# Gate and up of two feed-forward networks as a 2x2 block product by seven products

## The chip, the core and the metric

The kernel runs on one NeuronCore of a Trainium2 chip. Its engines are TensorE (PE in the profile; its weight loads are PEld), VectorE (DVE), ScalarE (ACT), GpSimd (POOL) and SyncE (SP, which here issues DMAs). Each has its own queue and works it in order. The metric is the time on the device in microseconds.

## The reference

One layer of a decoder for 512 tokens of 1024 features, in float32:

```python
x = x + 0.5 * RMSNorm(SwiGLU_1(RMSNorm(x)))
x = x + RMSNorm(mixer(RMSNorm(x)))        # attention and mLSTM, merged by gates
x = x + 0.5 * RMSNorm(SwiGLU_2(RMSNorm(x)))

def swiglu(x, w_gate, w_up, w_down):
    return (jax.nn.silu(x @ w_gate) * (x @ w_up)) @ w_down
```

w_gate and w_up are 1024 x 2816, w_down is 2816 x 1024. The change is in the two SwiGLUs.

## The kernel before

All runs on one core in program order: the first feed-forward network (a in the names), the mixer, the second one (b). Tokens lie along the free axis: hT holds the normed input, 1024 features as 8 chunks of 128 partitions by 512 tokens. Float32 accuracy is made from three products of rounded parts: each operand is split into a high part (h) and the rest (l), and xh·wh, xl·wh and xh·wl are added in PSUM.

`load_w` (L70 to L78) brings one weight tile of 128 x 1024 in: a DMA on SP's queue into wf (3 buffers), the high part wh by a cast on ScalarE (L75), the low part wl by a subtraction on VectorE (L77); wh and wl have 5 buffers each. `ws` (L165) makes one 128 x 512 output with 24 matmuls of 512 columns (8 chunks, three terms).

`ffn` runs over 22 blocks of 128 columns of gate and up. The first two (EARLY) go through `by_halves` (L175), in halves of 256 tokens, because the later tokens' norm is still under way. Each other block loads gate and up, runs `ws` for each, and `close` takes silu of gate on ScalarE (L228) and multiplies with up on VectorE (L229) into aT. Then `down` multiplies aT (split by `get_x` into ah, L250, and al, L251) with w_down, 22 steps of `step` (L215 to L217), and the post norm follows. GpSimd makes the power -1/2 of the norms (L89), a few masks at the start, and some DMAs.

The order of the work is that of the program as its scheduler places it by each tile's dependences; a tile with a number of buffers is free again when its last reader is done.

Of the kernel before, what the change touches and what calls it, by code (L numbers as in the profile page):

```python
# [39 lines left out]
def tile_hybrid_block(ctx: ExitStack, tc: tile.TileContext, a: dict):  # L40
# [180 lines left out]

    def ffn(pool, low, todo, first_w, hT, wgu, wd, post, finish, name, later=None, pins=()):
        hTh, hTl = hT
        aT = pool.tile([P, NF, T], F32, name=f"aT_{name}")

        def close(f, pg):
            s = pool.tile([P, T], F32, tag="s", bufs=2, name=f"s_{name}{f}")
            nc.scalar.activation(s, pg[0], AF.Silu)  # L228
            nc.vector.tensor_tensor(aT[:, f, :], pg[1], s, op=ALU.mult)  # L229
        early = []  # L230
        for f in range(EARLY):
            wg, wu = first_w if first_w and f == 0 else [load_w(wgu[f, b], f"{name}gu{f}{b}", after=pins if f + b else ()) for b in range(2)]
            early.append((wg, wu, pair(f"pg_{name}{f}")))
        by_halves([(pg, (wg, wu)) for wg, wu, pg in early], hTh, hTl, todo)
        for f in range(EARLY):
            close(f, early[f][2])
        if later:
            later()
# [15 lines left out]
        return down(pool, NF, lambda kk: wd[kk], get_x, post, finish, todo, name)  # L254


    with tc.tile_pool(name="low_a", bufs=1) as la, tc.tile_pool(name="ffn_a", bufs=1) as fa:
        hbuf = [(act, "h"), (fa, "h2")]
        tbuf = [(act, "tmp"), (fa, "tmp2")]
# [620 lines left out]
```

## Time and profile before

| | |
|---|---|
| median of 3 runs | 1408.47 us (1407.61 to 1408.63) |
| the profiled execution | 1408.52 us, its span 1406.7 us |
| busy TensorE, its weight loads | 99%, 84% |
| busy VectorE, ScalarE, GpSimd | 44%, 35%, 2% |
| mean granted clock of TensorE | 0.998 of full |

The busy shares are means over the whole span. A stretch is read by its own rows: how often a step comes back, and what ended each engine's idle time before it.

### The profile page before, as it was taken

What the parts mean: (1) busy time and instruction counts of PE and PEld (TensorE: products, weight loads), DVE (VectorE), ACT (ScalarE), POOL (GpSimd) and SP (SyncE); (2) the same over time, 40 slices, a digit from 0 to 9 for tenths busy, and PEclk for the clock granted to TensorE, in tenths of its full rate; (3) what the DMA queues carried; (4) which work ended last, traced back from release to release, by engine and by line L of the source; (5) the groups of instructions that cost most, each with busy time, mean ns of one, the idle gap of its engine ahead of it and who ended that gap; (6) DMA issues with size and microseconds to landing.
All of it is one profiled execution on the core that took longest, in us unless ns stands there. A gap on an engine that the chain in (4) does not pass through costs nothing.

```text
span 1406.7 us, 16599 instructions
## 1 busy us (share of the span) xinstructions
PE 1392.6 (99%) x6752; PEld 1185.3 (84%) x6752; DVE 625.0 (44%) x986; ACT 486.7 (35%) x761; POOL 29.1 (2%) x52
## 2 busy tenths in 40 slices
PE   8999999999999999999999999999999999999998
PEld 8888888888899889988888888888888888888886
DVE  5332222333773675565756753333374323222333
ACT  5322222222533533344445443222254222222322
POOL 1000000000100000000000000000010000000000
PEclk9999999999999999999999999999999999999999
DMA  6433333333143222222222232333323333323321
GB/s 234 126 90 100 96 102 92 93 103 91 46 121 115 90 76 75 75 75 75 75 87 78 75 118 78 90 101 95 105 76 120 91 104 90 103 92 97 99 75 60
DMA packets 37357, 133.12 MB, mean 95 GB/s; under 512 B 4268, under 2 KB 4268, under 8 KB 37280
## 3 DMA queue, kind: packets, MB, share of 16 engines
q1 hardware_dynamic: 36144, 128.50, 29.9%
q0 software_dynamic: 1136, 3.56, 0.8%
q8 instruction: 53, 0.87, 0.2%
q14 instruction: 24, 0.20, 0.0%
HBM read 129.95 MB, written 2.10 MB: 94 GB/s over the span
## 4 chain that ended last, share of the span: by engine, by line
PE 96%; DVE 1%; issue 1%; ACT 1%; DMA 0%; POOL 0%; SPq 0%; POOLq 0%; DVEq 0%; ACTq 0%
PE pg_b L165 15%; PE pg_a L165 15%; PE p L165 11%; PE pq L165 7%; PE pm L165 6%; PE acc_b L216 3%; PE acc_b L215 3%; PE acc_b L217 3%; PE acc_a L216 2%; PE acc_a L215 2%; PE acc_a L217 2%; PE pvo L602 2%; PE pvo L604 2%; PE pvo L603 2%; PE pg_a L175 2%; PE pq L175 2%
## 5 line engine op out<-in xcount | busy, mean ns | idle before, releaser
L215 PE MATMUL acc_a<-wh_ad,ah_a 128*128 128x512 f32 x176 | 68.6, 390 | 0.0
L217 PE MATMUL acc_a<-wl_ad,ah_a 128*128 128x512 f32 x176 | 68.5, 389 | 0.0
L216 PE MATMUL acc_a<-wh_ad,al_a 128*128 128x512 f32 x176 | 68.5, 389 | 0.0
L215 PE MATMUL acc_b<-wh_bd,ah_b 128*128 128x512 f32 x176 | 68.5, 389 | 0.0
L216 PE MATMUL acc_b<-wh_bd,al_b 128*128 128x512 f32 x176 | 68.5, 389 | 0.0
L217 PE MATMUL acc_b<-wl_bd,ah_b 128*128 128x512 f32 x176 | 68.5, 389 | 0.0
L165 PE MATMUL pq<-hTh_mx,wh_qk 128*128 128x512 f32 x160 | 63.5, 397 | 0.0
L165 PE MATMUL pq<-hTl_mx,wh_qk 128*128 128x512 f32 x160 | 62.4, 390 | 0.0
L165 PE MATMUL pg_a<-hTl_f,wh_ag 128*128 128x512 f32 x160 | 62.3, 389 | 0.0
L165 PE MATMUL pg_b<-hTl_f,wh_bg 128*128 128x512 f32 x160 | 62.3, 389 | 0.0
L165 PE MATMUL pg_a<-hTh_f,wh_ag 128*128 128x512 f32 x160 | 62.3, 389 | 0.0
L165 PE MATMUL pg_b<-hTh_f,wh_bg 128*128 128x512 f32 x160 | 62.3, 389 | 0.0
L165 PE MATMUL pg_a<-hTh_f,wh_au 128*128 128x512 f32 x160 | 62.2, 389 | 0.0
L165 PE MATMUL pg_a<-hTl_f,wh_au 128*128 128x512 f32 x160 | 62.2, 389 | 0.0
L165 PE MATMUL pg_b<-hTh_f,wh_bu 128*128 128x512 f32 x160 | 62.2, 389 | 0.0
L165 PE MATMUL pg_b<-hTl_f,wh_bu 128*128 128x512 f32 x160 | 62.2, 389 | 0.0
L77 DVE TENSOR_TENSOR wl_ad<-wf_ad,wh_ad 128x1024 fp32r<-128x1024 f32 x22 | 26.9, 1225 | 69.4 <-ACT wh_ad L75 69.4
L77 DVE TENSOR_TENSOR wl_bd<-wf_bd,wh_bd 128x1024 fp32r<-128x1024 f32 x22 | 26.9, 1225 | 69.4 <-ACT wh_bd L75 69.4
L77 DVE TENSOR_TENSOR wl_au<-wf_au,wh_au 128x1024 fp32r<-128x1024 f32 x20 | 24.5, 1226 | 69.7 <-ACT wh_au L75 63.6
L77 DVE TENSOR_TENSOR wl_bu<-wf_bu,wh_bu 128x1024 fp32r<-128x1024 f32 x20 | 24.5, 1226 | 69.7 <-ACT wh_bu L75 62.3
L229 DVE TENSOR_TENSOR aT_a<-pg_a,s_a 128x512 f32<-128x512 f32 x22 | 15.2, 691 | 85.3 <-PE pg_a L165 84.6
L229 DVE TENSOR_TENSOR aT_b<-pg_b,s_b 128x512 f32<-128x512 f32 x22 | 15.2, 691 | 84.6 <-PE pg_b L165 84.6
(339 smaller groups left out, 3432.9 us busy)
## 6 DMA issues: line engine op xcount, KB each, us to landing
wf_qk<-in_wqk SPq DMA_DIRECT2D x24, 512.0 KB, 3.6
wf_ad<-in_wd SPq DMA_DIRECT2D x22, 512.0 KB, 3.6
wf_bd<-in_wd SPq DMA_DIRECT2D x22, 512.0 KB, 3.6
wf_ag<-in_wgu SPq DMA_DIRECT2D x20, 512.0 KB, 3.6
wf_au<-in_wgu SPq DMA_DIRECT2D x20, 512.0 KB, 3.6
wf_bg<-in_wgu SPq DMA_DIRECT2D x20, 512.0 KB, 3.7
wf_bu<-in_wgu SPq DMA_DIRECT2D x20, 512.0 KB, 3.6
wf_mqk<-in_wmqk SPq DMA_DIRECT2D x16, 512.0 KB, 3.6
```

The source lines that it names most:

```text
L77: nc.vector.tensor_tensor(wl, wf, wh.bitcast(F32), op=ALU.subtract)
L165: nc.tensor.matmul(out, lhsT=wt[:, k * P:(k + 1) * P], rhs=x[:, k, tok], start=n == 0, stop=n == len(terms) - 1)
L175: nc.tensor.matmul(outs[b][:, tok], lhsT=ws_[b][w][:, k * P:(k + 1) * P], rhs=x[:, k, tok], start=i + k + hf == 0, stop=hf == 1 and i == 2 ...
L215: nc.tensor.matmul(out, lhsT=xh[:, tk], rhs=wh[:, cs], start=first, stop=False)
L216: nc.tensor.matmul(out, lhsT=xl[:, tk], rhs=wh[:, cs], start=False, stop=False)
L217: nc.tensor.matmul(out, lhsT=xh[:, tk], rhs=wl[:, cs], start=False, stop=last)
L229: nc.vector.tensor_tensor(aT[:, f, :], pg[1], s, op=ALU.mult)
L602: nc.tensor.matmul(out, lhsT=hTh[:, k, tk], rhs=wh[:, cs], start=k == 0, stop=False)
L603: nc.tensor.matmul(out, lhsT=hTl[:, k, tk], rhs=wh[:, cs], start=False, stop=False)
L604: nc.tensor.matmul(out, lhsT=hTh[:, k, tk], rhs=wl[:, cs], start=False, stop=k == KD - 1)
```

## The change

In blocks 4 to 21 of both networks (36 blocks) gate and up together become one 2x2 block product. One block's gate and up are the rows, two halves of the 1024 features are the inner blocks, and two halves of the 512 tokens the columns. Instead of 8 block products, 7 are made of sums of the weight blocks and sums of the token blocks. A product is 12 matmuls of 256 columns (4 chunks, three terms; `product`). I call them P1 to P7 by the number k in `product`; `g` and `u` are the weight tiles of a block, `a` to `d` their sums.

`token_parts` makes the sums of token blocks once per network, during block 2, in the part of aT that is written later. Per block, `front` has GpSimd make two sums (`ab`), `sums` has VectorE make two more (`cd`), and `take` splits each into h and l as `load_w` does: w1 and w2 from g, w4 from half of u, w6 and w3 from cd, w7 and w5 from ab. In the texts, wl12, wl4, wl63 and wl75 are the subtractions on VectorE for them. After the products VectorE joins them: `uv` (two sums in one), three `z`, and the product into aT; ScalarE copies `q1` and takes silu in two halves of 256 columns (silu0, silu1). Buffers: ab, cd, uv and s 1, z, q1 and w4 2, the other weights 5 as before. `Order` fixes the order on VectorE, ScalarE and GpSimd to the order of the calls. P4 of a block runs one turn late, between P5 and P2 of the next block. The gains' loads come after the blocks, and silu's s has 1 buffer.

```diff
@@ -219,44 +230,224 @@
+    Q = KD // 2 * P
+    H = T // 2
+    ADD, SUB, MUL = ALU.add, ALU.subtract, ALU.mult
...
+    class Order:
+        def __init__(self):
+            self.last = {}
+
+        def __call__(self, eng, fn, *args, **kw):
+            with tc.issue_after(self.last[eng]) if eng in self.last else nullcontext():
+                self.last[eng] = getattr(getattr(nc, eng), fn)(*args, **kw).ins
+
+    def token_parts(low, tmp, hTh, hTl, name):
+        def quad(t, i, j):
+            return t[:, 4 * i:4 * i + 4, j * H:(j + 1) * H]
+
+        hf, xs_ = tmp[:, 0:8, :], tmp[:, 8:16, :]
+        for j in (1, 0):
+            for i in (1, 0):
+                nc.vector.tensor_tensor(quad(hf, i, j), quad(hTh, i, j).bitcast(F32), quad(hTl, i, j).bitcast(F32),
+                                        op=ADD)
+        b11, b12, b21, b22 = (quad(hf, i, j) for i in range(2) for j in range(2))
+        f = {k: xs_[:, 2 * i:2 * i + 2, :].rearrange("p a (b c) -> p (a b) c", c=H) for i, k in enumerate((5, 6, 7, 4))}
+        parts = {1: (quad(hTh, 0, 0), quad(hTl, 0, 0)), 2: (quad(hTh, 1, 0), quad(hTl, 1, 0)),
+                 3: (quad(hTh, 1, 1), quad(hTl, 1, 1))}
+
+        def part(k):
+            xh, xl = (low.tile([P, 4, H], F32R, name=f"x{k}{x}_{name}") for x in "hl")
+            split(f[k], xh, xl)
+            parts[k] = (xh, xl)
+
+        nc.vector.tensor_tensor(f[5], b11, b12, op=SUB)
+        nc.vector.scalar_tensor_tensor(f[6], f[5], -1.0, b22, op0=MUL, op1=SUB)
+        part(6)
+        part(5)
+        nc.vector.tensor_tensor(f[7], b22, b12, op=SUB)
+        part(7)
+        nc.vector.scalar_tensor_tensor(f[4], f[6], -1.0, b21, op0=MUL, op1=SUB)
+        part(4)
+        return parts
+
+    def seven(fs, wgu, x, low, scr, aT, name):
+        do = Order()
+        tt = lambda out, p, q, op: do("vector", "tensor_tensor", out, p, q, op=op)
+        cast = lambda out, p: do("scalar", "copy", out, p)
+
+        class Unit:
+            def __init__(self, f):
+                self.f, self.n, self.w = f, f"{name}{f}", {}
+
+            def load(self):
+                self.gu = []
+                for b in range(2):
+                    t = act.tile([P, 2, Q], F32, tag="wf", bufs=3, name=f"{'gu'[b]}_{self.n}")
+                    nc.sync.dma_start(t, wgu[self.f, :, b * 1024:(b + 1) * 1024].rearrange("p (q c) -> p q c", c=Q))
+                    self.gu.append(t)
+
+            def take(self, keys, src, n=2):
+                pool, tag, bufs = (wpool, "", 5) if n == 2 else (low, "4", 2)
+                wh, wl = (pool.tile([P, n, Q], F32R, tag=f"w{y}{tag}", bufs=bufs, name=f"w{y}{keys[0]}_{self.n}")
+                          for y in "hl")
+                for i, k in enumerate(keys):
+                    self.w[k] = (wh[:, i, :], wl[:, i, :])
+                cast(wh, src)
+                return lambda: tt(wl, src, wh.bitcast(F32), SUB)
+
+            def front(self):
+                g, u = self.gu
+                self.ab = scr.tile([P, 2, Q], F32, tag="ab", bufs=1, name=f"ab_{self.n}")
+                do("gpsimd", "tensor_tensor", self.ab[:, 0, :], g[:, 0, :], u[:, 0, :], op=ADD)
+                do("gpsimd", "tensor_tensor", self.ab[:, 1, :], u[:, 0, :], u[:, 1, :], op=ADD)
+                self.low12 = self.take((1, 2), g)
+
+            def sums(self):
+                g, u = self.gu
+                cd = scr.tile([P, 2, Q], F32, tag="cd", bufs=1, name=f"cd_{self.n}")
+                low4 = self.take((4,), u[:, 1:2, :], 1)
+                tt(cd[:, 0, :], self.ab[:, 0, :], u[:, 1, :], ADD)
+                tt(cd[:, 1, :], cd[:, 0, :], g[:, 1, :], ADD)
+                self.lowcd = self.take((6, 3), cd)
+                low4()
+
+            def product(self, out, k, first, last):
+                (wh, wl), (xh, xl) = self.w[k], x[k]
+                terms = [(wh, y, i) for i in range(4) for y in (xh, xl)] + [(wl, xh, i) for i in range(4)]
+                for n, (wt, y, i) in enumerate(terms):
+                    nc.tensor.matmul(out, lhsT=wt[:, i * P:(i + 1) * P], rhs=y[:, i, :], start=first and n == 0,
+                                     stop=last and n == len(terms) - 1, skip_group_check=True)
+
+            def open(self):
+                n = self.n
+                self.pa, self.pb = bank(f"qa_{n}"), bank(f"qb_{n}")
+                self.q1 = scr.tile([P, H], F32, tag="q1", bufs=2, name=f"q1_{n}")
+                self.uv = scr.tile([P, 2, H], F32, tag="uv", bufs=1, name=f"uv_{n}")
+                self.z = scr.tile([P, 3, H], F32, tag="z", bufs=2, name=f"z_{n}")
+                self.s = scr.tile([P, 2, H], F32, tag="s", bufs=1, name=f"s_{n}")
+                self.a, self.b, self.c = self.pa[:, 0:H], self.pb[:, 0:H], self.pb[:, H:T]
+
+            def inner(self):
+                tt(self.z[:, 1, :], self.b, self.uv[:, 1, :], ADD)
+                tt(self.z[:, 2, :], self.c, self.uv[:, 0, :], ADD)
+
+            def silu(self, i):
+                do("scalar", "activation", self.s[:, i, :], self.z[:, 2, :] if i else self.a, AF.Silu)
+
+            def finish(self):
+                self.product(self.b, 4, False, False)
+                tt(self.z[:, 0, :], self.b, self.q1, ADD)
+                do("vector", "scalar_tensor_tensor", aT[:, self.f, :].rearrange("p (a b) -> p a b", b=H),
+                   self.z[:, 0:2, :], -1.0, self.s, op0=MUL, op1=MUL)
+
+        us = [Unit(f) for f in fs] + [None, None]
+        us[0].load()
+        us[0].front()
+        us[1].load()
+        us[0].low12()
+        us[0].sums()
+        us[0].lowcd()
+        us[0].take((7, 5), us[0].ab)()
+        us[1].front()
+        prev = None
+        for i in range(len(fs)):
+            u, v, w = us[i:i + 3]
+            u.open()
+            if prev:
+                prev.inner()
+                prev.silu(1)
+            u.product(u.a, 1, True, False)
+            cast(u.q1, u.a)
+            if v:
+                v.low12()
+            u.product(u.b, 6, True, False)
+            if w:
+                w.load()
+            if v:
+                v.sums()
+            u.product(u.c, 5, False, False)
+            tt(u.uv, u.pb.rearrange("p (a b) -> p a b", b=H), u.q1[:, None, :].broadcast_to([P, 2, H]), ADD)
+            if v:
+                v.lowcd()
+            if prev:
+                prev.finish()
+            u.product(u.a, 2, False, True)
+            u.silu(0)
+            if v:
+                v.take((7, 5), v.ab)()
+            u.product(u.b, 7, False, False)
+            u.product(u.c, 3, False, True)
+            if w:
+                w.front()
+            prev = u
+        prev.inner()
+        prev.silu(1)
+        prev.finish()
+
+    PLAIN = 4
...
-            s = pool.tile([P, T], F32, tag="s", bufs=2, name=f"s_{name}{f}")
...
-        for f in range(EARLY, NF):
-            wg = load_w(wgu[f, 0], f"{name}g{f}")
-            wu = load_w(wgu[f, 1], f"{name}u{f}")
-            pg = pair(f"pg_{name}{f}")
-            ws(pg[0], wg, KD, hTh, hTl)
-            ws(pg[1], wu, KD, hTh, hTl)
-            close(f, pg)
...
+            x = None
+            for f in range(EARLY, PLAIN):
+                w = load_plain(f)
+                if f == EARLY:
+                    x = token_parts(low, aT[:, NF - 16:, :], hTh, hTl, name)
+                pg = pair(f"pg_{name}{f}")
+                for b in range(2):
+                    ws(pg[b], w[b], KD, hTh, hTl)
+                close(f, pg)
+            seven(range(PLAIN, NF), wgu, x, low, scr, aT, name)
+
+        dn = ExitStack()
+        dlow = dn.enter_context(new_pool(f"low_{name}", "left"))
+        work.pool = dn.enter_context(new_pool(f"dn_{name}"))
+        if begin:
+            begin()
...
-        r[f"wgu{i}"] = np.stack([cols(f(f"{n}_w_gate")), cols(f(f"{n}_w_up"))], 1)
+        r[f"wgu{i}"] = np.concatenate([cols(f(f"{n}_w_gate")), cols(f(f"{n}_w_up"))], 2)
```

Three places of the new order. First VectorE in the middle of the first network, before: two weight subtractions and a product per block (ag9 is gate of block 9).

```order
L229 TENSOR_TENSOR aT_a_204<-pg_a6_1_724,s_a6_773 128x512
L77 TENSOR_TENSOR wl_ag9_910<-wf_ag9_906,wh_ag9_908 128x1024
L77 TENSOR_TENSOR wl_au9_916<-wf_au9_912,wh_au9_914 128x1024
L229 TENSOR_TENSOR aT_a_204<-pg_a7_1_789,s_a7_838 128x512
L77 TENSOR_TENSOR wl_ag10_975<-wf_ag10_971,wh_ag10_973 128x1024
```

The same engine and place now, one turn (wl1 is wl12, wl6 is wl63, wl7 is wl75; a7 to a9 are blocks):

```order
L247 TENSOR_TENSOR wl7_a8_1090<-ab_a8_993,wh7_a8_1089 128x1024
L247 TENSOR_TENSOR z_a7_1003<-qb_a7_1000,uv_a7_1002 128x256 x2
L247 TENSOR_TENSOR wl1_a9_1121<-g_a9_1034,wh1_a9_1120 128x1024
L247 TENSOR_TENSOR cd_a9_1162<-ab_a9_1117,u_a9_1036 128x512
L247 TENSOR_TENSOR cd_a9_1162<-cd_a9_1162,g_a9_1034 128x512
L247 TENSOR_TENSOR wl4_a9_1164<-u_a9_1036,wh4_a9_1163 128x512
L247 TENSOR_TENSOR uv_a8_1126<-qb_a8_1124,q1_a8_1125 128x512
L247 TENSOR_TENSOR wl6_a9_1169<-cd_a9_1162,wh6_a9_1168 128x1024
L247 TENSOR_TENSOR z_a7_1003<-qb_a7_1000,q1_a7_1001 128x256
L247 SCALAR_TENSOR_TENSOR aT_a_205<-z_a7_1003,s_a7_1004 128x512
L247 TENSOR_TENSOR wl7_a9_1214<-ab_a9_1117,wh7_a9_1213 128x1024
```

Each turn had three operations, and now has eleven: weight work of block 9 and the joining of blocks 7 and 8 alternate. Next ScalarE over the same turn, with what each row waits for (the s read from qa is silu0, that from z silu1):

```order
L247 ACTIVATE s_a7_1004<-qa_a7_999 128x256 [waits DVE_49,PE_49,Activation_49]
L247 CAST wh7_a8_1089<-ab_a8_993 128x1024 [waits Pool_49]
L247 CAST wh1_a9_1120<-g_a9_1034 128x1024 [waits DMAHW7_49,PE_49]
L247 ACTIVATE s_a7_1004<-z_a7_1003 128x256 [waits DVE_49]
L247 COPY q1_a8_1125<-qa_a8_1123 128x256 [waits PE_49]
L247 CAST wh4_a9_1163<-u_a9_1036 128x512 [waits DMAHW0_49,PE_49]
L247 CAST wh6_a9_1168<-cd_a9_1162 128x1024 [waits DVE_49]
```

Before, a turn was two casts and one silu. silu0 waits for VectorE, since s has one buffer and aT of the block before reads it; the cast of w4 waits for TensorE, since w4 has two. GpSimd, which had nothing to do in this stretch:

```order
L247 TENSOR_TENSOR ab_a8_993<-u_a8_912 128x512
L247 TENSOR_TENSOR ab_a9_1117<-g_a9_1034,u_a9_1036 128x512 [waits DMAHW7_49,DMAHW0_49,DVE_49]
L247 TENSOR_TENSOR ab_a9_1117<-u_a9_1036 128x512
```

The first add of a block waits for VectorE, the last reader of ab, which is wl75 of the block before. Last, VectorE at the end of the first network's blocks (d2 to d4 are weights of `down`, a21 is the last block):

```order
L88 TENSOR_TENSOR wl_ad2_2936<-wf_ad2_2932,wh_ad2_2934 128x1024
L88 TENSOR_TENSOR wl_ad3_2970<-wf_ad3_2966,wh_ad3_2968 128x1024
L247 TENSOR_TENSOR z_a21_2729<-qb_a21_2726,uv_a21_2728 128x256 x2
L88 TENSOR_TENSOR wl_ad4_3004<-wf_ad4_3000,wh_ad4_3002 128x1024
L247 TENSOR_TENSOR z_a21_2729<-qb_a21_2726,q1_a21_2727 128x256
L247 SCALAR_TENSOR_TENSOR aT_a_205<-z_a21_2729,s_a21_2730 128x512
L438 TENSOR_TENSOR al_a0_2853<-aT_a_205,ah_a0_2852 128x512
```

Weights of down stand between the last block's steps, and al of step 0 stands behind them all; before, al of the first steps was made early, among the blocks.

## Rows read from the trace of the kernel before

**Rows 1.** The page's head, busy time of each engine, and its chain by engine.

```profile
span 1406.7 us, 16599 instructions
PE 1392.6 (99%) x6752; PEld 1185.3 (84%) x6752; DVE 625.0 (44%) x986; ACT 486.7 (35%) x761; POOL 29.1 (2%) x52
...
PE 96%; DVE 1%; issue 1%; ACT 1%; DMA 0%; POOL 0%; SPq 0%; POOLq 0%; DVEq 0%; ACTq 0%
```

**Rows 2.** Timeline, VectorE: start, length (us), engine, line, operation, tiles, count.

```profile
49.29 0.69 DVE L229 TENSOR_TENSOR aT_a<-pg_a,s_a 128x512 f32<-128x512 f32 x1 [4.23 <-PE pg_a L165]
49.90 1.22 DVE L77 TENSOR_TENSOR wl_ag<-wf_ag,wh_ag 128x1024 fp32r<-128x1024 f32 x1
51.03 0.69 DVE L251 TENSOR_TENSOR al_a<-aT_a,ah_a 128x512 fp32r<-128x512 f32 x1
...
60.17 0.69 DVE L229 TENSOR_TENSOR aT_a<-pg_a,s_a 128x512 f32<-128x512 f32 x1 [4.23 <-PE pg_a L165]
...
71.05 0.69 DVE L229 TENSOR_TENSOR aT_a<-pg_a,s_a 128x512 f32<-128x512 f32 x1 [4.22 <-PE pg_a L165]
```

**Rows 3.** Windows: busy us (count) of PE, PEld, DVE, ACT, POOL; clock, DMA.

```profile
20.00:40.00 20.00, 20.00 (x163) 19.66 (x162) 11.59 (x14) 10.51 (x14) 0.34 (x1) 1.00 0.52 162
50.00:70.00 20.00, 20.00 (x90) 16.57 (x89) 6.59 (x7) 6.42 (x8) 0.00 (x0) 1.00 0.34 106
```

**Rows 4.** Timeline, TensorE, the halves of the first two blocks.

```profile
30.43 2.08 PE L175 MATMUL pg_a<-hTh_f,wl_agu 128*128 128x256 f32 x16
32.35 2.08 PE L175 MATMUL pg_a<-hTh_f,wh_agu 128*128 128x256 f32 x16
```

**Rows 5.** Groups by form, VectorE: busy us, mean ns, then idle before.

```profile
L755 DVE SCALAR_TENSOR_TENSOR t<-t,p 128x512 f32<-128x512 f32 x16 | 11.0, 688 | 42.7 <-PE p L165 42.7
L612 DVE TENSOR_TENSOR vml<-pvo,vmh 128x256 fp32r<-128x256 f32 x16 | 6.7, 420 | 0.0
```

**Rows 6.** Groups by form, ScalarE.

```profile
L75 ACT CAST wh_au<-wf_au 128x1024 fp32r<-128x1024 f32 x18 | 18.9, 1047 | 70.3 <-PE pg_a L165 70.3
L250 ACT CAST ah_a<-aT_a 128x512 fp32r<-128x512 f32 x20 | 12.3, 615 | 4.7 <-DVE aT_a L229 4.7
...
L676 ACT ACTIVATE jm<-po,dn 128x256 f32<-128x256 f32 x16 | 7.5, 472 | 4.3 <-DVE dn L673 4.1
L611 ACT CAST vmh<-pvo 128x256 fp32r<-128x256 f32 x16 | 6.0, 373 | 2.3 <-PE pvo L604 2.2
```

**Rows 7.** Timeline, TensorE, the end of block 2.

```profile
47.66 1.52 PE L165 MATMUL pg_a<-hTh_f,wl_au 128*128 128x512 f32 x6
```

**Rows 8.** Timeline, VectorE and TensorE, the first transposes.

```profile
6.58 0.75 DVE L129 SCALAR_TENSOR_TENSOR h_f<-x,r_f,g_f1pre 128x512 f32<-128x512 f32 x1 [0.93 <-DMA g_f1pre<-in_ffn_pre_g]
...
7.47 0.63 PE L137 MATMUL pt_f<-ident,h_f 128*128 128x128 f32 x4 [1.57 <-DVE h_f L129]
```

**Rows 9.** Timeline, GpSimd, the start.

```profile
0.24 0.10 POOL L869 MEMSET const-float32-0.0<- 128x1 f32 x1 [0.24 <-issue]
...
0.74 0.20 POOL masks.py:197 MEMSET ident<- 128x128 f32 x1 [0.29 <-POOLq L869]
1.02 0.29 POOL masks.py:199 TENSOR_SCALAR_AFFINE_SELECT ident<-ident 128x128 f32<-128x128 f32 x1
```

**Rows 10.** Timeline, VectorE and GpSimd, the post norm of the first network.

```profile
360.08 0.16 DVE L100 SCALAR_TENSOR_TENSOR v_pf<-sp_f 128x1 f32<-128x1 f32 x1 [2.09 <-ACT jk_pf L96]
360.15 0.69 DVE L154 TENSOR_TENSOR fg_f<-acc_a,g_f1post 128x512 f32<-128x512 f32 x1
...
360.40 0.56 POOL L89 TENSOR_TENSOR r_pf<-v_pf,nhalf 128x1 f32<-128x1 f32 x1 [340.06 <-DVE v_pf L100]
```

**Rows 11.** Timeline, VectorE, the last pre norm before the mixer.

```profile
383.45 0.15 DVE L100 SCALAR_TENSOR_TENSOR v_mx<-ss_mx 128x1 f32<-128x1 f32 x1
383.52 1.21 DVE L77 TENSOR_TENSOR wl_qk<-wf_qk,wh_qk 128x1024 fp32r<-128x1024 f32 x1
385.18 0.49 DVE L117 TENSOR_SCALAR h_mx<-h_mx,r_mx 128x512 f32<-128x512 f32 x1 [0.44 <-POOL r_mx L89]
```

**Rows 12.** Timeline, GpSimd, the same place.

```profile
383.68 1.46 POOL L89 TENSOR_TENSOR r_mx<-v_mx,nhalf 128x1 f32<-128x1 f32 x1 [4.91 <-DVE v_mx L100]
```

**Rows 13.** Timeline, TensorE, from the last block to down.

```profile
254.83 1.07 PE L165 MATMUL pg_a<-hTh_f,wl_au 128*128 128x512 f32 x4
255.74 0.39 PE L215 MATMUL acc_a<-wh_ad,ah_a 128*128 128x512 f32 x1
```

**Rows 14.** DMA issues: count, KB each, median us to landing.

```profile
wf_ag<-in_wgu SPq DMA_DIRECT2D x20, 512.0 KB, 3.6
```

More of the change, by code (lines that the diff above doesn't have):

```diff
@@ L47, in tile_hybrid_block, with new_pool, tile @@
     act = ctx.enter_context(tc.tile_pool(name="act", bufs=1, side="right"))
+    def new_pool(name, side="right"):
+        return tc.tile_pool(name=name, bufs=1, side=side, reuse_waits="tile")
+    class Work:
+        pool = None
+        def tile(self, *args, **kw):
+            return self.pool.tile(*args, **kw)
+    work = Work()
     small = ctx.enter_context(tc.tile_pool(name="small", bufs=4, side="right"))
@@ L80, in gain @@
     def gain(src, name, eng=None):
-        g = act.tile([P, D], F32, tag="gain", bufs=2, name=f"g_{name}")
+        g = work.tile([P, D], F32, tag="gain", bufs=2, name=f"g_{name}")
         (eng or nc.gpsimd).dma_start(g, src.partition_broadcast(P))
@@ L220, in flush, with split @@
         return todo.pop(0)() if todo else None
-    def ffn(pool, low, todo, first_w, hT, wgu, wd, post, finish, name, later=None, pins=()):
+    Q = KD // 2 * P
+    H = T // 2
+    ADD, SUB, MUL = ALU.add, ALU.subtract, ALU.mult
+    def split(src, wh, wl):
+        nc.scalar.copy(wh, src)
+        nc.vector.tensor_tensor(wl, src, wh.bitcast(F32), op=SUB)
+    class Order:
[4 more added lines that the diff above has]
+                self.last[eng] = getattr(getattr(nc, eng), fn)(*args, **kw).ins
@@ L223, in ffn @@
+    PLAIN = 4
+    def ffn(pool, todo, first_w, hT, wgu, wd, post, finish, name, begin=None, pins=()):
         hTh, hTl = hT
         aT = pool.tile([P, NF, T], F32, name=f"aT_{name}")
-        def close(f, pg):
-            s = pool.tile([P, T], F32, tag="s", bufs=2, name=f"s_{name}{f}")
[L228 to L238, printed above, removed]
-        for f in range(EARLY, NF):
-            wg = load_w(wgu[f, 0], f"{name}g{f}")
-            wu = load_w(wgu[f, 1], f"{name}u{f}")
-            pg = pair(f"pg_{name}{f}")
-            ws(pg[0], wg, KD, hTh, hTl)
-            ws(pg[1], wu, KD, hTh, hTl)
-            close(f, pg)
+        with ExitStack() as st:
+            low = st.enter_context(new_pool(f"parts_{name}", "left"))
+            scr = st.enter_context(new_pool(f"gu_{name}"))
+            def close(f, pg):
+                s = scr.tile([P, 2, H], F32, tag="s", bufs=1, name=f"s_{name}{f}").rearrange("p a b -> p (a b)")
+                nc.scalar.activation(s, pg[0], AF.Silu)
+                nc.vector.tensor_tensor(aT[:, f, :], pg[1], s, op=MUL)
+            def load_plain(f):
+                return [load_w(wgu[f, :, b * 1024:(b + 1) * 1024], f"{name}gu{f}{b}",
+                               after=pins if f < EARLY and f + b else ()) for b in range(2)]
+            early = []
+            for f in range(EARLY):
+                w = first_w if first_w and f == 0 else load_plain(f)
+                early.append((*w, pair(f"pg_{name}{f}")))
+            by_halves([(pg, (wg, wu)) for wg, wu, pg in early], hTh, hTl, todo)
+            for f in range(EARLY):
+                close(f, early[f][2])
+            x = None
[8 more added lines that the diff above has]
+            seven(range(PLAIN, NF), wgu, x, low, scr, aT, name)
@@ L252, in get_x @@
             return ah, al
[L254 to L259, printed above, removed]
+        pins = down(pool, NF, lambda kk: wd[kk], get_x, post, finish, todo, name)
+        dn.close()
+        return pins
+    with new_pool("ffn_a") as fa:
+        hbuf = [(work, "h"), (work, "h2")]
+        tbuf = [(work, "tmp"), (work, "tmp2")]
+        op_ctx = ExitStack()
+        work.pool = op_ctx.enter_context(new_pool("opening"))
         def load_x(t):
@@ L270, in tile_hybrid_block @@
             turned = pins[0]
-        first_w = [load_w(a["wgu1"][0, b], f"agu0{b}", after=pins if b else ()) for b in range(2)]
+        first_w = [load_w(a["wgu1"][0, :, b * 1024:(b + 1) * 1024], f"agu0{b}", after=pins if b else ()) for b in range(2)]
         todo = []
@@ L300, in tile_hybrid_block @@
     mctx = ExitStack()
+    work.pool = mctx.enter_context(new_pool("work"))
     mix = mctx.enter_context(tc.tile_pool(name="mix", bufs=1, side="right"))
@@ L519, in tile_hybrid_block @@
     ones4, Gm = gc4[:, 0, :], gc4[:, 1, :]
-    selr = act.tile([4, D], F32R, tag="gain", bufs=2, name="selr")
+    selr = work.tile([4, D], F32R, tag="gain", bufs=2, name="selr")
     Gh = selr[:, 512:1024]
@@ L778, in tile_hybrid_block @@
     mctx.close()
-    g_post2 = gain(a["ffn2_post_g"], "f2post")
-    with tc.tile_pool(name="low_b", bufs=1) as lb, tc.tile_pool(name="ffn_b", bufs=1) as fb:
+    g_post2 = []
+    with new_pool("ffn_b") as fb:
         def post3(t):
-            return PostNorm(t, g_post2, [(act, "tmp"), (fb, "tmp2")][t % 2], "f2", True)
+            return PostNorm(t, g_post2[0], [(work, "tmp"), (work, "tmp2")][t % 2], "f2", True)
         def finish3(t):
```

32 lines of the change are left out of this document (17 added, 15 removed).

## The prediction

> **What bounds the kernel now.** I read the page's head first. TensorE is busy 99% of a span of 1406.7 us, VectorE 44%, ScalarE 35%, GpSimd 2%, and the chain that ended last is TensorE for 96% [rows 1]. So time is TensorE's work, as long as the other engines feed it. Next VectorE's timeline inside a gate/up stretch: the product that closes a block starts at 49.29, 60.17 and 71.05 [rows 2]. A block therefore takes 10.88 us; its 48 matmuls of 512 columns follow each other every 0.227 us, with nothing waited for. In that stretch 20 us hold 6.6 us of VectorE and 6.4 us of ScalarE [rows 3], so both have slack. The granted clock is 1.00 in the stretches shown, the 2.4 GHz level. The sum below is made against the profiled execution, 1408.52 us (span and 1.8 us around it); the median of the runs is 1408.47, the same to 0.05 us. A measurement of this kernel tells about 0.2%, or 2.8 us, from no change.
>
> **What the matmuls save.** A changed block has 7 products of 12 matmuls with 256 columns: 84 in place of 48. The same shape runs in the first two blocks: groups of 16 start 1.92 us apart, 0.120 us each [rows 4], with the weight loads busy 19.66 of 20 us [rows 3]. So 84 x 0.120 = 10.08 us against 10.88. Over 18 blocks of one FFN that is 181.4 against 195.8 us, and over both FFNs 28.8 us if nothing else moves. This is only 7% of a block, so a wait of 0.8 us per block eats all of it.
>
> **What feeds a block now.** Before, VectorE had three or four operations per block and each looked far ahead. Now there are eleven. By rows: three of 128x1024 at 1.13 us start to start, two sums, wl4 and uv at 0.61 (all four 128x512), three z of 128x256 at 0.42, and the aT product at 0.69 [rows 2, 5]: 7.8 us. ScalarE has three casts of 1.05, one of 0.62, a copy of 0.37 and two silus of 0.47 [rows 5, 6]: 5.1 us. Both fit in 10.08 us, so the busy shares don't decide; the order does. I follow two circles.
>
> *Circle through w4.* The cast of w4 for the next block waits for the eighth matmul of P4 of the block before, because w4 has two buffers. P4 begins 2.88 us into a turn. Its eighth matmul starts at 3.72 and lasts 0.28 (16 take 2.08, the starts 1.80 [rows 4]); a reader of PSUM starts 0.10 after a matmul's end (47.66 + 1.52 = 49.18 to 49.29 [rows 7, 2]). Cast 4.10 to 4.72, wl4 4.76 to 5.37, uv to 6.06, and P7 may start 0.14 later: 6.20, where TensorE is ready at 6.00 (50 matmuls into the turn). The hop of 0.14 is from VectorE's h_f (6.58 + 0.75) to the first transpose at 7.47 [rows 8]. That is 0.2 us per turn, a turn of 10.28.
>
> *Circle through ab.* The buffers ab, cd and s are single. GpSimd may write ab for the next block only when wl75 has read it; VectorE's sum cd0 waits for GpSimd's first add; and wl75 waits for its cast, which is queued on ScalarE behind silu0, which waits for aT of the block before. This closes a circle that runs once a turn without TensorE in it. GpSimd's new cost is the unknown. The trace has no 128x512 add there. It has a memset of one column (0.10), of 128 columns (0.20) and a select that reads and writes 128 (0.29) [rows 9]: 0.8 ns per column for a write, 0.7 more for a read. A second read at the same price makes 2.2 ns, so 0.10 + 512 x 2.2 ns = 1.23 us an add, an estimate. If the second read were free it would be 0.87; if the one-input slope doubled, 1.65. I take 1.23, the one that counts its three streams alike.
>
> Whether the adds run beside VectorE is the second unknown, and it decides the sign. Rows: the rsqrt power on GpSimd takes 0.56 us while VectorE runs a product with one input in PSUM (360.15, for 0.69) [rows 10]. It takes 1.46 us at 383.68, while VectorE runs a 128x1024 subtraction with both inputs in SBUF (383.52 to 384.73) [rows 11, 12]. GpSimd was thus held until that subtraction ended. No row shows VectorE held by GpSimd; between none and the whole add I take the whole, since the same resource must be free for both. The Trainium skill (SBUF — State Buffer, "Who interferes with whom") states this rule, which speaks against the change: a VectorE instruction with two SBUF inputs and a GpSimd instruction that reads SBUF exclude each other, and the second to issue waits for the whole of the first. The trace agrees for GpSimd as the second (1.46 against 0.56 us); no run here shows the reverse.
>
> So the circle: wl75 ends; 0.16 until GpSimd starts (360.24 to 360.40 [rows 10]); first add 1.23, under which VectorE does z1 and z2 (one input in PSUM); wl12 with two SBUF inputs stands blocked and then takes 1.13; the second add, waiting longest, goes next, 1.23; cd0 and cd1, each needing the one before it whole, 0.69 each; wl4 and uv 0.61 each, which cover cd's cast; wl63 1.13; z0 0.42; aT 0.69; silu0 0.47; cast 1.05; wl75 1.22; two hops of 0.04. Sum 11.41 us, longer than the block before. TensorE then waits 11.41 - 10.08 = 1.33 us per turn, at P7, whose uv comes late. There are 16 turns per FFN with an add in them; the first starts with its sums made ahead, so 15 x 1.33 = 20.0 us.
>
> The Trainium skill (GPSIMD Engine Reference, "3.1 Elementwise — side-by-side cycle accounting") gives 4497 ns for an add of 2048 fp32 columns, by which I estimate 1.12 us for 512; the time would then come out near 1418. No run here shows that operation.
>
> **The end of the seven-product stretch.** Down began without a gap before (255.74 follows the last wl_au matmul [rows 13]). Now, on VectorE, the low part of down's fourth weight stands ahead of z1 and z2 of the last block, and its cast waits for the eighth matmul of P7. From P3's start: cast -0.22 to 0.83, subtraction 0.87 to 2.00, two z to 2.84, P4 at 2.98 instead of 1.44: 1.5 us. Then al of step 0 waits for z0, aT and the split: P4 ends at 4.42, reader at 4.68, 0.42 + 0.69 + 0.68, hop 0.14, so 6.61, while TensorE has only six matmuls of 0.227 to do: 0.8 us. Together 2.4 us per FFN. Afterwards ah and al run ahead again.
>
> **Edits at nothing.** The token parts (four sums, four differences, four splits, all 128x1024, some 14 us of VectorE) are hidden by blocks 2 and 3 (21.8 us of TensorE) and what is left of the halves; without that cover each costs its 1.1 us once. The gains' loads on GpSimd's queue go out after the adds, 100 us before they are read. A weight load lands 3.6 us after its issue [rows 14]; on SP's queue, u waits for cd1 of the block before and has some 5 us over; if it were late, GpSimd's first add would be next.
>
> **Sum.** One FFN: 181.4 + 20.0 + 2.4 = 203.8 against 195.8, +8.0; two: +16.0. 1408.5 + 16.0 = **1424.5 us**. With the add at 1.05 to 1.40 us this case reaches from 1414 to 1435.
>
> **Rivals.**
> 1. *The adds cost VectorE nothing.* Only the first add is then on the circle and z1, z2 and wl12 (1.97) cover it; the circle falls below 10 us and the w4 circle sets 10.28. One FFN: 181.4 + 16 x 0.2 + 2.4 = 187.0, -8.8; both -17.6: 1391. For it: no row shows VectorE slowed, and the powers beside PSUM products weren't held. Against it: the 1.46. It decides if wl12, cd0 and cd1 keep 1.13 and 0.61 to 0.69 beside an add. Chance 0.34.
> 2. *The second add slips.* VectorE keeps going through wl12, cd0, cd1 and wl4; the add runs under uv and holds wl63 for 1.23 - 0.61 = 0.62. Turn 11.41 - 1.23 + 0.62 = 10.80, FFN 194.6, time 1406: no change. For it: subtractions start before the one ahead has ended (1.13 apart, 1.22 long), so a stream of them may leave no gap. Against it: cd1 waits for cd0, and in that gap the add comes first. An add of 0.87 with all blocked gives 10.69 and 1403. Chance 0.14.
> 3. *The add takes 1.65 us or more*, blocked: 12.25 a turn, FFN 216.4, 1450. Chance 0.07.
>
> **How the numbers follow.** The forecast has 0.45, and 1424.5 is its time. Faster takes rival 1 and a little of rival 2: 0.36. Same: most of rival 2 and the forecast's lowest end: 0.13. Slower: the rest, 0.51. The range must reach to rival 1, whose price hangs on hops of 0.1 us in 32 turns (3 us), so from 1388; its top is the forecast's own, 1435. That leaves out rival 3 and the tails.
>
> **What would show it.** Right: the closing aT product on VectorE every 11.4 us; TensorE idle some 1.3 us a block before x7, released by uv; GpSimd's two adds with a subtraction between them; cd0 released by GpSimd. Rival 1: aT every 10.2 to 10.3 us, idle 0.2. Rival 2: 10.8, and wl63 starting late beside an add. The forecast is wrong at its root if 128x1024 subtractions that stand beside an add keep 1.22 us and start on time, or if TensorE's granted clock falls below 1.00 after its waits, which no row here prices.

## The result, and the profile after

The changed kernel takes 1412.08 us (median of 11 runs, 1411.16 to 1413.47) against 1408.63 us for the kernel before, run beside it (11 runs): a ratio of 1.0026, 95% interval 1.0017 to 1.0035. It is slower, by 3.5 us; 16 were forecast, and 1424.5 us was the predicted time. The way was right and the size was not. One run of e4 below took 4800.57 us and is left out of that experiment's figures.

The head of its page and its chain by engine, which answer to [rows 1]:

```profile
span 1409.4 us, 19843 instructions
PE 1372.8 (97%) x8048; PEld 1224.4 (87%) x8048; DVE 879.3 (62%) x1298; ACT 562.3 (40%) x913; POOL 153.7 (11%) x124
...
PE 71%; DVE 19%; issue 5%; ACT 3%; DMA 1%; POOL 0%; DVEq 0%; ACTq 0%; SPq 0%; POOLq 0%
```

TensorE is 20 us less busy, and the span is 2.7 us longer. The chain now runs through VectorE for 19% of the span. No engine but TensorE is near full: this is a chain of waits, not a lack of capacity.

Its VectorE timeline over one turn answers to [rows 2], where a block took 10.88 us. The rows are, in order: wl75, z1 with z2, wl12, cd0, cd1, wl4, uv, wl63, z0, aT, and wl75 of the next turn.

```profile
101.05 1.23 DVE L247 TENSOR_TENSOR wl_a<-ab_a,wh_a 128x1024 fp32r<-128x1024 f32 x1 [1.47 <-ACT wh_a L247]
102.19 0.75 DVE L247 TENSOR_TENSOR z_a<-qb_a,uv_a 128x256 f32<-128x256 f32 x2
102.86 1.87 DVE L247 TENSOR_TENSOR wl_a<-g_a,wh_a 128x1024 fp32r<-128x1024 f32 x1
104.65 1.78 DVE L247 TENSOR_TENSOR cd_a<-ab_a,u_a 128x512 f32<-128x512 f32 x1
106.47 0.69 DVE L247 TENSOR_TENSOR cd_a<-cd_a,g_a 128x512 f32<-128x512 f32 x1
107.08 0.68 DVE L247 TENSOR_TENSOR wl_a<-u_a,wh_a 128x512 fp32r<-128x512 f32 x1
107.68 0.68 DVE L247 TENSOR_TENSOR uv_a<-qb_a,q_a 128x512 f32<-128x512 f32 x1
108.28 1.22 DVE L247 TENSOR_TENSOR wl_a<-cd_a,wh_a 128x1024 fp32r<-128x1024 f32 x1
109.41 0.42 DVE L247 TENSOR_TENSOR z_a<-qb_a,q_a 128x256 f32<-128x256 f32 x1
109.86 0.69 DVE L247 SCALAR_TENSOR_TENSOR aT_a<-z_a,s_a 128x512 f32<-128x512 f32 x1
112.02 1.23 DVE L247 TENSOR_TENSOR wl_a<-ab_a,wh_a 128x1024 fp32r<-128x1024 f32 x1 [1.47 <-ACT wh_a L247]
```

The turn is 112.02 - 101.05 = 10.97 us. Across the first network aT starts at 76.92 and, 15 turns later, at 241.62: 10.98 each. Two operations are long: the 128x1024 subtraction from g (wl12) shows 1.87 us where the others take 1.23, and the 128x512 sum cd0 1.78 where cd1 takes 0.69. GpSimd at the same place:

```profile
102.36 1.29 POOL L247 TENSOR_TENSOR ab_a<-g_a,u_a 128x512 f32<-128x512 f32 x1 [7.45 <-DVE wl_a L247]
103.60 2.28 POOL L247 TENSOR_TENSOR ab_a<-u_a 128x512 f32<-128x512 f32 x1
```

The first add runs until the second is issued at 103.60; wl12 then needs its usual 1.13 and ends at 104.73. The second add, shown from 103.60, ends at 105.88; cd0 ends 0.55 later, at 106.43. So VectorE and GpSimd take turns, add, wl12, add, cd0, each held until the other is done. The two z beside the first add take 0.75 for both: they have one input in PSUM and aren't held.

That this is a hold, and not two engines that slow each other, the first block of the seven-product stretch shows. There VectorE stands idle beside the first add, and cd0 is issued just behind the second:

```profile
46.11 1.30 POOL L247 TENSOR_TENSOR ab_a<-g_a,u_a 128x512 f32<-128x512 f32 x1 [28.21 <-DMA u_a<-in_wgu]
47.37 1.28 POOL L247 TENSOR_TENSOR ab_a<-u_a 128x512 f32<-128x512 f32 x1
47.44 1.75 DVE L247 TENSOR_TENSOR cd_a<-ab_a,u_a 128x512 f32<-128x512 f32 x1 [1.87 <-POOL ab_a L247]
```

The add takes 1.30 alone, 1.28 with cd0 waiting, and 1.29 above with wl12 waiting: the one that was issued first isn't slowed, and cd0 ends 0.54 after the add does.

ScalarE, the link between aT and the next wl75 (group and columns as above):

```profile
110.67 0.39 ACT L247 ACTIVATE s_a<-qa_a 128x256 f32<-128x256 f32 x1 [2.43 <-DVE aT_a L247]
110.95 1.04 ACT L247 CAST wh_a<-ab_a 128x1024 fp32r<-128x1024 f32 x1
```

silu0 is released by aT, the cast follows 0.28 after its start, and VectorE meanwhile stands idle 1.47 us, the figure in the brackets above. Last TensorE: the first matmul of P7 with its neighbours, and the waits summed over the run (total us, times, longest).

```profile
107.49 0.28 PE L323 MATMUL qa_a<-hTl_f,wh_a 128*128 128x256 f32 x1
108.41 0.39 PE L323 MATMUL qb_a<-x7h_a,wh_a 128*128 128x256 f32 x1 [0.65 <-DVE uv_a L247]
108.64 0.28 PE L323 MATMUL qb_a<-x7l_a,wh_a 128*128 128x256 f32 x1
```

```profile
PE qb_a L323 <- DVE uv_a L247: 9.7, 15, 0.7
PE qb_b L323 <- DVE uv_b L247: 9.7, 15, 0.7
PE pt_f L148 <- DVE h_f L140: 2.1, 2, 1.7
PE qb_b L323 <- DVE z_b L247: 1.7, 1, 1.7
PE qb_a L323 <- DVE z_a L247: 1.1, 1, 1.1
```

P7 waits for uv 15 times per network, as the forecast had it. The matmul before starts at 107.49, so P7 could start at 107.61; it starts 0.80 us later, and its second matmul follows after 0.23 in place of 0.12. That is 0.9 us a turn, which is the turn's 10.98 less the 10.08 of its matmuls.

### The profile page after: what moved, and what is told of

The parts are those of the page before. It is cut to its first block, busy times and chain, and to the rows that moved or that the text cites. A ratio compares the mean times of both kernels' runs of the same rounds, so it can differ in the third digit from the quotient of the medians.

```text
span 1409.4 us, 19843 instructions
## 1 busy us (share of the span) xinstructions
PE 1372.8 (97%) x8048; PEld 1224.4 (87%) x8048; DVE 879.3 (62%) x1298; ACT 562.3 (40%) x913; POOL 153.7 (11%) x124
## 3 DMA queue, kind: packets, MB, share of 16 engines
q1 hardware_dynamic: 36144, 128.50, 27.4%
## 4 chain that ended last, share of the span: by engine, by line
PE 71%; DVE 19%; issue 5%; ACT 3%; DMA 1%; POOL 0%; DVEq 0%; ACTq 0%; SPq 0%; POOLq 0%
PE p L176 11%; PE pq L176 7%; PE pm L176 6%; DVE wl_b L247 4%; DVE wl_a L247 4%; PE acc_a L227 3%; PE acc_a L228 3%; PE acc_a L226 3%; PE acc_b L227 3%; PE acc_b L228 3%; PE acc_b L226 3%; PE pvo L795 2%; PE pvo L796 2%; PE pvo L797 2%; DVE cd_b L247 2%
## 5 line engine op out<-in xcount | busy, mean ns | idle before, releaser
L88 DVE TENSOR_TENSOR wl_qk<-wf_qk,wh_qk 128x1024 fp32r<-128x1024 f32 x24 | 29.3, 1221 | 47.5 <-ACT wh_qk L86 33.9
L86 ACT CAST wh_bd<-wf_bd 128x1024 fp32r<-128x1024 f32 x22 | 23.0, 1050 | 71.0 <-PE acc_b L227 66.7
L176 PE MATMUL pm<-hTh_mx,wh_mqk 128*128 128x512 f32 x128 | 50.4, 394 | 0.0
L795 PE MATMUL pvo<-wh_vo,hTh_mx 128*128 128x512 f32 x128 | 50.2, 392 | 0.0
L176 PE MATMUL pm<-hTl_mx,wh_mqk 128*128 128x512 f32 x128 | 49.9, 390 | 0.0
L176 PE MATMUL p<-hTh_mx,wh_gm 128*128 128x512 f32 x128 | 49.9, 390 | 0.0
L797 PE MATMUL pvo<-wl_vo,hTh_mx 128*128 128x512 f32 x128 | 49.8, 389 | 0.0
L176 PE MATMUL p<-hTl_mx,wh_gm 128*128 128x512 f32 x128 | 49.8, 389 | 0.0
L796 PE MATMUL pvo<-wh_vo,hTl_mx 128*128 128x512 f32 x128 | 49.8, 389 | 0.0
L86 ACT CAST wh_qk<-wf_qk 128x1024 fp32r<-128x1024 f32 x24 | 25.0, 1051 | 54.0 <-PE pw L543 28.8
```

The source lines that it names most:

```text
L86: nc.scalar.copy(wh, wf)
L88: nc.vector.tensor_tensor(wl, wf, wh.bitcast(F32), op=ALU.subtract)
L176: nc.tensor.matmul(out, lhsT=wt[:, k * P:(k + 1) * P], rhs=x[:, k, tok], start=n == 0, stop=n == len(terms) - 1)
L795: nc.tensor.matmul(out, lhsT=hTh[:, k, tk], rhs=wh[:, cs], start=k == 0, stop=False)
L796: nc.tensor.matmul(out, lhsT=hTl[:, k, tk], rhs=wh[:, cs], start=False, stop=False)
L797: nc.tensor.matmul(out, lhsT=hTh[:, k, tk], rhs=wl[:, cs], start=False, stop=k == KD - 1)
```

## The experiments

Theory A is the forecast's: the turn is a circle through the single buffers (wl75, ab, wl12, cd, wl4, uv, wl63, z0, aT, silu0, cast, wl75), in which each add holds VectorE. Its rivals are that the rest of the change costs something, that VectorE is long for reasons of its own, that VectorE is just too full, and that the circle through w4's buffers sets the turn. The kernel before took 1408.3 to 1408.6 us in these runs.

**e1, no seven-product block.**

```diff
-    PLAIN = 4
+    PLAIN = NF
-                if f == EARLY:
-                    x = token_parts(low, aT[:, NF - 16:, :], hTh, hTl, name)
-            seven(range(PLAIN, NF), wgu, x, low, scr, aT, name)
```

> All 22 blocks of both networks go the plain way; token_parts and seven are not called, the pools, the weight layout and the moved gain loads of the change stay. Theory A (the seven-product blocks alone carry the difference: 10.98 us a turn against 10.88, plus about 2 us at the end of each network): 1408.5 us, within 1.5 us of the kernel before, blocks back at 10.88 us. Rival (the new pools or the moved loads cost something too): 1410 to 1412 us.

Measured: 1406.96 us, ratio 0.9993 (0.9984 to 1.0003). The pools, the weight layout and the moved loads cost nothing that can be measured; what the change does to the time is in the blocks.

**e2, the adds on VectorE.**

```diff
-                do("gpsimd", "tensor_tensor", self.ab[:, 0, :], g[:, 0, :], u[:, 0, :], op=ADD)
-                do("gpsimd", "tensor_tensor", self.ab[:, 1, :], u[:, 0, :], u[:, 1, :], op=ADD)
+                do("vector", "tensor_tensor", self.ab[:, 0, :], g[:, 0, :], u[:, 0, :], op=ADD)
+                do("vector", "tensor_tensor", self.ab[:, 1, :], u[:, 0, :], u[:, 1, :], op=ADD)
```

> The two sums ab go to VectorE; GpSimd does nothing in the blocks, VectorE gets 1.2 us more work a turn. Theory A (the turn is the circle wl75, ab, wl12, cd, ..., silu0, cast, wl75, and each add on GpSimd holds VectorE): from the end of wl75 to the start of cd0's own work 3.6 us become 2 x 0.61 + 0.67 + 1.13 = 3.0, the turn 10.98 becomes about 10.3 us, time 1392 us, wl12 back at 1.22 us and cd0 at 0.69. Rival (the long wl12 and cd0 come from VectorE itself or from another engine, not from GpSimd): the turn grows by 1.2 to about 12.2 us, 1448 us, and wl12 stays at 1.87.

Measured: 1397.69 us, ratio 0.9927 (0.9912 to 0.9942). VectorE's timeline of this kernel, the place of wl12 and cd0:

```profile
122.12 1.23 DVE L247 TENSOR_TENSOR wl_a<-ab_a,wh_a 128x1024 fp32r<-128x1024 f32 x1 [1.47 <-ACT wh_a L247]
123.38 0.69 DVE L247 TENSOR_TENSOR ab_a<-g_a,u_a 128x512 f32<-128x512 f32 x1
123.99 0.68 DVE L247 TENSOR_TENSOR ab_a<-u_a 128x512 f32<-128x512 f32 x1
124.59 0.75 DVE L247 TENSOR_TENSOR z_a<-qb_a,uv_a 128x256 f32<-128x256 f32 x2
125.26 1.22 DVE L247 TENSOR_TENSOR wl_a<-g_a,wh_a 128x1024 fp32r<-128x1024 f32 x1
126.39 0.69 DVE L247 TENSOR_TENSOR cd_a<-ab_a,u_a 128x512 f32<-128x512 f32 x1
...
132.67 1.23 DVE L247 TENSOR_TENSOR wl_a<-ab_a,wh_a 128x1024 fp32r<-128x1024 f32 x1 [1.46 <-ACT wh_a L247]
```

wl12 and cd0 are back at 1.22 and 0.69: the length came from GpSimd. VectorE has 1.2 us more work and the turn is shorter, 10.55 us. From wl75's end to cd0's start it is 3.04 us, as expected (3.0), where the changed kernel has 3.60 to cd0's own work: 0.56 less. The turn fell by 0.43, since 0.13 of that comes back: an unheld cd0 needs 0.72 to the start of cd1, the held one 0.59 from the end of the add (105.88 to 106.47). The 10.3 on record were 10.98 - 0.6, rounded down. That is the ab circle without GpSimd.

**e3, silu in two buffers.**

```diff
-                self.z = scr.tile([P, 3, H], F32, tag="z", bufs=2, name=f"z_{n}")
-                self.s = scr.tile([P, 2, H], F32, tag="s", bufs=1, name=f"s_{n}")
+                self.z = scr.tile([P, 4, H], F32, tag="z", bufs=2, name=f"z_{n}")
+                self.s = self.z[:, 2:4, :]
-                tt(self.z[:, 2, :], self.c, self.uv[:, 0, :], ADD)
+                tt(self.z[:, 3, :], self.c, self.uv[:, 0, :], ADD)
-                do("scalar", "activation", self.s[:, i, :], self.z[:, 2, :] if i else self.a, AF.Silu)
+                do("scalar", "activation", self.s[:, i, :], self.z[:, 3, :] if i else self.a, AF.Silu)
```

The silu of the plain blocks goes into the same tile (that line isn't shown).

> silu's halves go into the two-buffer tile of z (of four parts, silu1 in place), the same memory; silu0 no longer waits for aT of the block before. Adds stay on GpSimd. Theory A: the 1.47 us in which VectorE waits for wl75's cast fall out of the circle, it drops to about 9.5 us, and the w4 circle sets 10.25 us; 1389 to 1391 us, wait before P7 about 0.1 to 0.2 us. Rival (VectorE with the holding of the adds is simply too full, 9.5 us of work and holding a turn, any shift is eaten): 1408 to 1412 us.

Measured: 1389.37 us, ratio 0.9866 (0.9850 to 0.9883). VectorE's timeline of this kernel, from wl12 to the next:

```profile
122.08 1.88 DVE L247 TENSOR_TENSOR wl_a<-g_a,wh_a 128x1024 fp32r<-128x1024 f32 x1
123.89 1.78 DVE L247 TENSOR_TENSOR cd_a<-ab_a,u_a 128x512 f32<-128x512 f32 x1
125.70 0.69 DVE L247 TENSOR_TENSOR cd_a<-cd_a,g_a 128x512 f32<-128x512 f32 x1
127.10 0.69 DVE L247 TENSOR_TENSOR wl_a<-u_a,wh_a 128x512 fp32r<-128x512 f32 x1 [0.71 <-ACT wh_a L247]
...
129.89 0.69 DVE L247 SCALAR_TENSOR_TENSOR aT_a<-z_a 128x512 f32<-128x512 f32 x1
130.50 1.22 DVE L247 TENSOR_TENSOR wl_a<-ab_a,wh_a 128x1024 fp32r<-128x1024 f32 x1
...
132.30 1.88 DVE L247 TENSOR_TENSOR wl_a<-g_a,wh_a 128x1024 fp32r<-128x1024 f32 x1
```

The holding is all still there (1.88, 1.78), the 1.47 ahead of wl75 is gone, and the turn is 10.22 us: now VectorE waits 0.71 for the cast of w4, the other circle, where the prediction's working had put it (10.28). VectorE is held as long as in the changed kernel and the turn is shorter all the same: VectorE was not too full.

**e4, uv ahead of wl4.** The edit keeps `low4` in the block and calls it after uv (and, not shown, once ahead of the first turn):

```diff
-                low4()
+                self.low4 = low4
...
             if v:
+                v.low4()
                 v.lowcd()
```

> Only the place of wl4 in VectorE's order changes: behind uv instead of ahead of it, so P7 no longer hangs on w4's buffers. Theory A (the ab circle, in which wl4 and uv both lie whichever is first, sets the turn): turn stays at 10.98 us, time 1411 to 1412 us; the wait only moves from P7 to a later product. Rival (the w4 circle, with uv queued behind wl4, sets the turn): 0.2 to 0.6 us less a turn, 1393 to 1406 us.

Measured: 1410.90 us (median of the other nine runs), ratio 1.0021 (1.0011 to 1.0030), against 1.0026 (1.0017 to 1.0035) of the changed kernel. wl75 in two turns, and the wait at P7:

```profile
122.89 1.23 DVE L247 TENSOR_TENSOR wl_a<-ab_a,wh_a 128x1024 fp32r<-128x1024 f32 x1 [1.47 <-ACT wh_a L247]
...
133.87 1.23 DVE L247 TENSOR_TENSOR wl_a<-ab_a,wh_a 128x1024 fp32r<-128x1024 f32 x1 [1.47 <-ACT wh_a L247]
```

```profile
PE qb_a L323 <- DVE uv_a L247: 9.2, 15, 0.7
```

The turn is still 10.98 us, and the gain is within the spread: the w4 circle is not what sets the turn. The text on record had the wait move to a later product. It did not: it stayed at P7 (9.2 us in 15 waits per network), since uv is on the ab circle in either place.

**e5, both e3 and e4.**

> The edit of e3 (silu in the two-buffer tile of z) and that of e4 (uv ahead of wl4) together. Theory A: with the ab circle at about 9.5 us, the w4 circle is what is left (10.22 us in e3); with uv out of its queue the turn falls to TensorE's own 10.08 us, so 32 turns save another 0.14: 1385 us, and no wait before P7. Rival (e4 moved nothing, so uv's place is worth nothing here either): 1389.4 us as e3.

Measured: 1384.66 us, ratio 0.9832 (0.9818 to 0.9845). The same edit that brought nothing alone brings 4.7 us over e3 once the ab circle is open. The windows over 180 us of the first network's blocks, first of the changed kernel, then of e5 (columns as in [rows 3]):

```profile
60.00:240.00 180.00, 170.47 (x1390) 167.35 (x1389) 151.45 (x177) 75.71 (x115) 56.50 (x32) 1.00 0.29 94
```

```profile
60.00:240.00 180.00, 180.00 (x1496) 179.76 (x1495) 163.06 (x191) 81.65 (x124) 56.48 (x32) 1.00 0.33 106
```

TensorE has no gap left, and aT comes back every 10.08 us (78.67 to 229.86 in 15 turns), the figure of [rows 4]. The clock is 1.00 in both, so the waits didn't change it.

**e6, a third add on GpSimd** (the second written twice, same values).

```diff
                 do("gpsimd", "tensor_tensor", self.ab[:, 1, :], u[:, 0, :], u[:, 1, :], op=ADD)
+                do("gpsimd", "tensor_tensor", self.ab[:, 1, :], u[:, 0, :], u[:, 1, :], op=ADD)
```

> The changed kernel with GpSimd's second add written twice, to the same place with the same values. Theory A (each add holds VectorE for its whole length inside the circle): the turn grows by one add, 1.18 us, to 12.15 us; 1447 us. Rival (only the wait of cd0 for the first add counts, the second runs beside VectorE): 1412 us, turn 10.98.

Measured: 1441.56 us, ratio 1.0235 (1.0221 to 1.0249). VectorE in this kernel:

```profile
130.70 1.88 DVE L247 TENSOR_TENSOR wl_a<-g_a,wh_a 128x1024 fp32r<-128x1024 f32 x1
132.50 1.78 DVE L247 TENSOR_TENSOR cd_a<-ab_a,u_a 128x512 f32<-128x512 f32 x1
134.32 1.67 DVE L247 TENSOR_TENSOR cd_a<-cd_a,g_a 128x512 f32<-128x512 f32 x1
```

GpSimd beside it, the two last adds in one row:

```profile
130.20 1.30 POOL L247 TENSOR_TENSOR ab_a<-g_a,u_a 128x512 f32<-128x512 f32 x1 [6.71 <-DVE wl_a L247]
131.46 3.98 POOL L247 TENSOR_TENSOR ab_a<-u_a 128x512 f32<-128x512 f32 x2
```

Now cd1 is held too: 1.67 in place of 0.69. So each add does hold VectorE, and it goes between two operations of VectorE, one at a time. The price is 0.98, not the 1.18 I gave it: the third add runs 1.16, from cd0's end at 134.28 to 135.44, and cd1 then ends 0.55 later, where unheld it ends 0.73 after cd0 (106.43 to 107.16). The turn is 11.95 us.

**e7, e5 with the adds on VectorE** (the edit of e2).

> e5 with the adds on VectorE, GpSimd idle in the blocks. Theory A: VectorE has 9.1 us of work a turn and no holding, the circle is below 10.08 us as in e5, so the time is that of e5, 1385 us within 1 us: once off the circle it does not matter which engine adds. Rival (VectorE needs the relief once TensorE runs at its own pace): 1388 to 1395 us.

Measured: 1384.34 us, ratio 0.9829 (0.9816 to 0.9842), the same as e5. Once the ab circle has slack it makes no difference which engine adds.

**e8, e5 with `PLAIN = 3`.**

> e5 with 3 plain blocks in place of 4 per network, 38 blocks by seven products. One block more per network saves 0.8 us each, 1.6 us; against it VectorE has 10.9 us less of cover for the token parts at the start, where it was busy almost without a gap from 20 to 45 us. Theory A: 1383 to 1386 us. Rival (the token parts are no longer hidden): a wait of some us at the first turn of each network, 1387 us or more.

Measured: 1383.33 us, ratio 0.9823 (0.9810 to 0.9837), the fastest here, 25 us under the kernel before. Against e5 it is 1.3 us, and the spreads of the two touch (1384.13 the lowest of e5, 1384.41 the highest of e8): the token parts still find cover with one plain block less, and more than that the runs don't settle.

## Why the prediction was wrong

Right, each with its run: the seven products at 0.120 us a matmul (e5, 10.08 us a turn); the circle and its order, with the wait at P7 behind uv in 15 turns per network; the add on GpSimd at 1.23 us (1.24 from issue to issue); VectorE and GpSimd holding each other for whole instructions (e2, e6); products with an input in PSUM not held; the w4 circle near 10.28 (10.22 in e3); no cost in the pools and the moved loads (e1). The rule of the Trainium skill (SBUF — State Buffer, "Who interferes with whom") is that the second to issue waits for the whole of the first. Its half that no run had shown is now measured and agrees: VectorE, second to issue, waited from 102.86 to 103.60 for an add that began at 102.36, and GpSimd then for wl12. From the add price of the Trainium skill (GPSIMD Engine Reference, "3.1 Elementwise — side-by-side cycle accounting") I had estimated 1.12 us; it is 1.24 here, and the measurement decides. The 1418 us that the estimate gave lie nearer to the result only because other terms of the sum were too long.

The step that failed is the sum of the circle, 11.41 us, which measured 10.97. Term by term, each measured from the rows above:

| term | on record | measured |
|---|---|---|
| wl75's end to GpSimd | 0.16 | 0.08 |
| first add | 1.23 | 1.24 |
| wl12 | 1.13 | 1.13 |
| second add | 1.23 | 1.15 |
| cd0, cd1 | 1.38 | 0.55 + 0.65 |
| wl4, uv, wl63 | 2.35 | 2.33 |
| z0, aT | 1.11 | 1.14 |
| aT to silu0 | 0.04 | 0.12 |
| silu0 | 0.47 | 0.28 |
| cast, hop | 1.09 | 1.07 |
| wl75 | 1.22 | 1.23 |
| sum | 11.41 | 10.97 |

For silu0 I took a length, 0.47 (that of another activation; silu0 itself shows 0.39), though the cast behind it on the same engine starts 0.28 after it; for cd0 and cd1 two full lengths, where a held operation needs only 0.55 after the hold ends. Those are 0.19 and 0.18 us. The first hop and the second add were 0.08 each too long, and the hop to silu0 0.08 too short. But 0.44 us in 15 turns of two networks is 13.2 us, and the forecast missed by 12.4. What was forecast is the difference between two nearly equal numbers, a turn of 11.41 against one of 10.88, and an error of 4% of the turn took 0.44 of those 0.53 us. That the sign still came out is in part luck: the measured turn is only 0.10 us longer than the block that it replaced, less than a quarter of the sum's error. The range of the forecast's own case, from 1414, was drawn from the add's price alone, the term that came out right; the sum of the other links had no bounds, and should have had some. The wider range held the time only because it reached across to rival 1.

The sum with the measured turn: one network 181.4 + 15 x 0.90 + 2.4 = 197.3 against 195.8, and two networks +3.0 us, where 3.5 were measured. The end of the stretch was about as priced. TensorE stood idle 1.1 us ahead of the last P4 in the first network and 1.7 in the second, and 0.53 ahead of al of step 0 in both:

```profile
254.29 0.39 PE L323 MATMUL qb_a<-x4h_a,wh_a 128*128 128x256 f32 x1 [1.15 <-DVE z_a L247]
...
257.91 0.50 PE L227 MATMUL acc_a<-wh_ad,al_a 128*128 128x512 f32 x1 [0.53 <-DVE al_a L438]
```

Counted from start to start, as on record, that is 1.4 and 1.9 us for P4 (1.5 on record) and 0.8 for al (0.8 on record), 4.9 us for both networks.

So the 28.8 us that the matmuls save were earned and then given back: 27 us to the circle (30 turns of 0.90) and some 5 to the waits at the two ends. e5 opens both circles, and 27.4 us come back.

## What to carry to other kernels

Where a wait comes back in every turn, look for the circle: follow the single buffers across the engines until they close, and sum it link by link. It need not hold the engine that is busiest, and one more buffer in the right place (here none, only another layout of the same memory) can be worth more than the work that the change saved. In such a sum take an operation's start-to-start time to the next one behind it, not its length, wherever the next one doesn't wait for its result; and before forecasting a sign, compare the sum's likely error, times the turns, with the margin. A helper engine whose instructions hold those of the engine that it relieves can cost more than it takes off: with the adds on GpSimd the turn is 10.98 us, with them on VectorE 10.55 (e2). Where the circle has slack it makes no difference (e5, e7).

## What the runs showed of the hardware that was not expected

A held instruction starts in the profile when it is issued, not when it runs: wl12 shows 1.87 us and GpSimd's second add 2.28, though neither did more than 1.13 and 1.15 us of work. So their busy shares (VectorE 62%, GpSimd 11%) contain the waiting, and a length above that of the same operation elsewhere is the sign of it. And the order of issue decides who goes: in the rows shown, of two instructions that exclude each other the one that was issued first runs, and the other waits for its end. Where each engine's next one is already waiting, this makes them alternate (add, wl12, add, cd0, and with a third add: add, cd1, in e6).
